# The recurrence's gates in the first mixer: issued behind each pair of convolutions, in main PSUM banks, with tanh and a second exponential

## The chip, the cores and the metric

One core of one Trainium2 chip runs the program. The metric is device time in microseconds (us), the median of three runs. PE is the matmul engine, DVE the vector engine, ACT the engine of activation functions, POOL the general one (GpSimd), SP the queue that issues loads.

## The reference

Two decoder layers on 256 tokens of width 1024, all in float32. Layer 0 has a mixer of two branches (a gated linear recurrence, RG-LRU, and sliding-window attention) and a dense SwiGLU; layer 1 has a gated DeltaNet and a mixture of 8 experts. The change lies in the recurrence of layer 0, whose width is 512:

```python
xc = causal_depthwise_conv(xb, conv_w) + conv_b          # width 4
r  = sigmoid(blockdiag(w_a) @ xc + b_a)
gi = sigmoid(blockdiag(w_i) @ xc + b_i)
log_a = -8 * r * softplus(-lam)
a  = exp(log_a)
u  = sqrt(-expm1(2 * log_a)) * (gi * xc)
h[t] = a[t] * h[t-1] + u[t]                              # scan over tokens
y_lru = h * gelu(gate)
```

The attention branch takes q, k and v from the same input projection; both branches feed one output projection.

## The kernel before, in words

Activations stand channels by tokens. Every float32 operand is split in two parts (`split`, L165 to L167): ACT rounds a copy (`hi`, L166) and DVE subtracts it (`lo`, L167); a product is then three fast matmuls (`mm3`, L220). Weights arrive in tiles of 1 MB and are split the same way, one ACT and one DVE instruction of 128x2048 each. Two `hi` buffers hold the split weights in turn, so the split of the next tile but one waits until PE has done with the older tile.

The input projection of layer 0 runs as six items in the order `kv x0 x1 qq g0 g1` (`L0ORD`): keys and values, the two halves of the recurrence's input, queries, the two halves of its output gate. `x0` and `x1` are 48 matmuls of 256 columns each (`chan_unit`), `qq` is 48 of 512 columns. The result of `x0` holds two of the recurrence's four blocks of 128 channels (blocks 0 and 1), that of `x1` blocks 2 and 3. Each block goes through `conv`: one ACT Identity (L400) and three DVE taps (L402) into the tile `xc`. Here "gate" means the pair of small block-diagonal products of one block (`wgate`), and not the items `g0` and `g1`.

Smaller chains are generators in the list `sides`; `pump` advances them between matmuls. In the kernel before, `lru_side` joins that list when both halves are convolved: per block it issues the gate's two matmuls into a bank of the four `ps` banks, two Sigmoids, later the Exp and Tanh, products on POOL, one Sqrt over all blocks, products on POOL, and the scan on DVE (L603). Its result times the GeLU gate `ge` is split into `yth` and `ytl`, which the output projection reads first. A scheduler places all instructions on their engines' queues by priority and by its own estimates of time, so that the order on a queue is not that of the source. `xc`, `rr`, `gi`, `aa` and `th_` are whole tiles for all four blocks. The tiles of matrix results are `pm` (four main banks, from `mbank`) and `ps` (four side banks, from `bank`).

Of the kernel before, what the change touches and what calls it, by code (L numbers as in the profile page):

```python
# [62 lines left out]
def body(ctx, tc, T, out, hrows):  # L63
# [357 lines left out]
    with tc.tile_pool(name="l0", bufs=1) as lp:  # L421
# [156 lines left out]

        def lru_side():
            for i in range(HB):  # L580
                b = bank([P, 2, S])
                for g in range(2):
                    mm(b[:, g, :], wgate[:, g, i, :], xc[:, i, :], True, True)
                nc.scalar.activation(rr[:, i, :], b[:, 0, :], AF.Sigmoid, bias=lruc[:, i, 5:6])
                sig = nc.scalar.activation(gi[:, i, :], b[:, 1, :], AF.Sigmoid, bias=lruc[:, i, 6:7])
                if i < HB - 1:
                    yield
            with tc.issue_after(sig.ins):
                for i in range(HB):
                    nc.scalar.activation(aa[:, i, :], rr[:, i, :], AF.Exp, scale=spn[:, i:i + 1])  # L590
                    nc.scalar.activation(th_[:, i, :], rr[:, i, :], AF.Tanh, scale=spp[:, i:i + 1])
            yield
            for i in range(HB):
                nc.gpsimd.tensor_tensor(gi[:, i, :], gi[:, i, :], xc[:, i, :], ALU.mult)
                nc.gpsimd.tensor_tensor(rr[:, i, :], aa[:, i, :], aa[:, i, :], ALU.mult)
                nc.vector.scalar_tensor_tensor(th_[:, i, :], rr[:, i, :], 1.0, th_[:, i, :], op0=ALU.add, op1=ALU.mult)
                if i % 2:
                    yield
            nc.scalar.activation(th_, th_, AF.Sqrt)
            yield  # L600
            for i in range(HB):
                nc.gpsimd.tensor_tensor(gi[:, i, :], gi[:, i, :], th_[:, i, :], ALU.mult)
                nc.vector.tensor_tensor_scan(xc[:, i, :], aa[:, i, :], gi[:, i, :], 0.0, op0=ALU.mult, op1=ALU.add)  # L603
                if i % 2:
                    yield
            while not {"g0", "g1"} <= done:
                yield
            for u in range(2):
                sl = slice(2 * u, 2 * u + 2)
                nc.vector.scalar_tensor_tensor(ge[:, sl], ge[:, sl], 0.5, xc[:, sl], op0=ALU.mult, op1=ALU.mult)  # L610
# [7 lines left out]
        nc.vector.tensor_scalar(spn, sp, -8.0, None, op0=ALU.mult)  # L618
        spp = lp.tile([P, HB], F32, name="spp")
        nc.vector.tensor_scalar(spp, sp, 8.0, None, op0=ALU.mult)  # L620
        done = set()
        for item in L0ORD.split():
# [9 lines left out]
            elif item[0] == "x":  # L632
                b = chan_unit(hnT)
                for m in range(2):
                    i = 2 * u + m
                    conv(b[:, m, :], lruc[:, i, 0:4], xc[:, i, :], bias=lruc[:, i, 4:5])
                done.add(item)
# [834 lines left out]
```

## Time and profile before

| what | value |
|---|---|
| median of 3 runs | 1514.45 us (1514.42 to 1515.34) |
| the profiled execution, its own time | 1516.59 us |
| its span, first to last instruction | 1514.5 us |
| mean granted TensorE clock | 0.982 |
| PE busy | 1470.5 us, 97% of the span |
| ACT, DVE, POOL busy | 950.1, 1178.7, 124.3 us |

A timeline row reads: start, duration, engine, line, operation, output <- inputs, shapes, how many instructions are merged in the row, and in brackets how long the engine had been idle before it and which instruction ended that. The granted clock is a share of full speed; 1.00 is 2.4 GHz, 0.50 is 1.2 GHz.

### The profile page before, as it was taken

The numbers are of one execution on the slowest core, as the hardware profiler recorded it, in microseconds if no ns is written. First come the engines' busy times: TensorE is split into PE (matmuls) and PEld (weight loads), VectorE is DVE, ScalarE is ACT, GpSimd is POOL, SyncE is SP. The second block draws the span as 40 slices with busy tenths as digits, with TensorE's granted clock in tenths as the row PEclk, the third lists the DMA queues.
The fourth block names the chain that finished last, engine by engine and source line by source line (L and its number), as shares of the span: only waits on it lengthen the run. The fifth ranks groups of instructions, "written<-read, shape, count | busy, mean of one in ns | idle before, by whom it ended". The sixth has DMA issues, their size and how long they took to land. (4 is left out here: it accounts for less than half of the span.)

```text
span 1514.5 us, 19426 instructions
## 1 busy us (share of the span) xinstructions
PE 1470.5 (97%) x7702; PEld 1246.4 (82%) x7702; DVE 1178.7 (78%) x1030; ACT 950.1 (63%) x894; POOL 124.3 (8%) x168
## 2 busy tenths in 40 slices
PE   8899999989998999999999999999999999999997
PEld 7679999969987778888888888888888888888886
DVE  5855444466867678888888888888898888888886
ACT  5744434345645467667767677767777667776674
POOL 2500000042010020010000000001001001001000
PEclk9899999989999899999999999999999999999999
DMA  8124455433330788999999999999999999999991
GB/s 319 68 111 154 172 190 188 180 140 112 140 138 4 300 324 344 373 357 391 375 370 383 367 372 382 379 372 376 383 365 372 386 372 358 391 375 370 385 355 17
DMA packets 65617, 435.79 MB, mean 288 GB/s; under 512 B 8304, under 2 KB 9584, under 8 KB 14320
## 3 DMA queue, kind: packets, MB, share of 16 engines
q1 hardware_dynamic: 62208, 426.62, 73.4%
q0 software_dynamic: 3312, 7.87, 2.2%
q8 instruction: 62, 1.02, 0.3%
q14 instruction: 35, 0.29, 0.0%
HBM read 428.17 MB, written 6.29 MB: 287 GB/s over the span
## 5 line engine op out<-in xcount | busy, mean ns | idle before, releaser
L220 PE MATMUL pm<-hi,X 128*128 128x512 f32 x1776 | 577.7, 396 | 0.0
L166 ACT ACTIVATE hi<-raw_raw 128x2048 fp32r<-128x2048 f32 (+2 forms) x199 | 352.4, 1810 | 146.1 <-PE pm L220 102.7
L167 DVE TENSOR_TENSOR lo_raw<-raw_raw,hi 128x2048 fp32r<-128x2048 f32 (+2 forms) x150 | 318.2, 2127 | 123.4 <-ACT hi L166 118.0
L220 PEld LDWEIGHTS pm<-hi,X 128*128 128x128 f32 x1776 | 333.6, 188 | 74.1
L167 DVE TENSOR_TENSOR lo_mraw<-raw_mraw,hi 128x2048 fp32r<-128x2048 f32 (+1 forms) x157 | 348.6, 2222 | 38.5 <-ACT hi L166 29.5
L166 ACT ACTIVATE hi<-raw_mraw 128x2048 fp32r<-128x2048 f32 (+1 forms) x186 | 330.3, 1852 | 0.0
L220 PE MATMUL ps<-hi,mG 128*128 128x512 f32 x864 | 277.9, 392 | 0.0
L220 PE MATMUL pm<-lo_mraw,X 128*128 128x512 f32 x496 | 193.9, 393 | 0.0
L220 PEld LDWEIGHTS ps<-hi,mG 128*128 128x128 f32 x864 | 162.2, 188 | 37.2
L220 PE MATMUL pm<-thi,hi 128*128 128x256 f32 x608 | 173.7, 286 | 1.2 <-ACT thi L166 1.2
L220 PE MATMUL pm<-tlo,hi 128*128 128x256 f32 x608 | 173.7, 286 | 0.3 <-DVE tlo L167 0.3
L220 PE MATMUL pm<-thi,lo_raw 128*128 128x256 f32 x592 | 169.2, 286 | 0.0
L1262 ACT ACTIVATE ms<-pm 128x512 f32<-128x512 f32 x56 | 33.5, 597 | 208.5 <-PE pm L220 172.5
L220 PE MATMUL pm<-lo_raw,X 128*128 128x512 f32 x348 | 136.8, 393 | 0.0
L220 PEld LDWEIGHTS pm<-thi,hi 128*128 128x128 f32 x608 | 118.0, 194 | 3.1 <-ACT thi L166 1.5
L220 PEld LDWEIGHTS pm<-tlo,hi 128*128 128x128 f32 x608 | 117.9, 194 | 1.7 <-DVE tlo L167 0.6
L220 PEld LDWEIGHTS pm<-thi,lo_raw 128*128 128x128 f32 x592 | 114.9, 194 | 0.7 <-issue 0.5
L220 PEld LDWEIGHTS pm<-lo_mraw,X 128*128 128x128 f32 x496 | 93.3, 188 | 19.6
L220 PE MATMUL ps<-lo_mraw,mG 128*128 128x512 f32 x268 | 100.8, 394 | 0.7 <-ACT mG L166 0.7
L1277 POOL DMA_INDIRECT out<-Y,si x16 | 29.9, 1868 | 635.2 <-ACT Y L1276 634.5
L220 PEld LDWEIGHTS pm<-lo_raw,X 128*128 128x128 f32 x348 | 65.5, 188 | 13.7
L220 PE MATMUL ps<-lo_raw,mG 128*128 128x512 f32 x180 | 70.8, 393 | 0.0
(376 smaller groups left out, 1815.4 us busy)
## 6 DMA issues: line engine op xcount, KB each, us to landing
raw_mraw<-in_moe SPq DMA_DIRECT2D x182, 1024.0 KB, 6.0
raw_raw<-in_moe SPq DMA_DIRECT2D x127, 1024.0 KB, 6.3
raw_tlo<-in_moe SPq DMA_DIRECT2D x26, 1024.0 KB, 6.5
raw_raw<-in_w SPq DMA_DIRECT2D x21, 1024.0 KB, 5.0
raw_raw<-in_fg SPq DMA_DIRECT2D x11, 1024.0 KB, 4.8
raw_raw<-in_fu SPq DMA_DIRECT2D x11, 1024.0 KB, 4.8
raw_raw<-in_fd SPq DMA_DIRECT2D x11, 1024.0 KB, 4.8
raw_raw<-in_w0o SPq DMA_DIRECT2D x4, 1024.0 KB, 4.8
```

The lines of the kernel that those rows point to most:

```text
L166: a = nc.scalar.activation(hi, src, AF.Copy)
L167: return a.ins, nc.vector.tensor_tensor(lo, src, hi.bitcast(F32), ALU.subtract).ins
L220: pe_last[0] = nc.tensor.matmul(o, l, r, start=start, stop=stop).ins
L1262: nc.scalar.activation(s, b, AF.Silu)
L1277: nc.gpsimd.indirect_dma_start(out[n], bass.IndirectOffsetOnAxis(ap=si, axis=0), Y[:, sl], None, bounds_check=ROWS - 1, oob_is_err=True, c ...
```

## The change

`lru_gates(i)` replaces the first half of `lru_side`. It is called for both blocks of a half right behind their convolutions, at a raised priority (`SPRI` is 20). Its matmuls write to main banks. Sigmoid(v) is written as (1 + tanh(v/2))/2; the factors of one half go into the constants (`spn`, `spp`, `hb`, the 0.25 at the end). The squared decay, before a product on POOL, is a second exponential. The products with `xc` and with the root go to DVE.

```diff
--- before.py
+++ after.py
@@ -576,30 +576,24 @@
         th_ = lp.tile([P, HB, S], F32, name="th_")
         ge = lp.tile([P, HB, S], F32, name="ge")
 
+        def lru_gates(i):
+            b = mbank([P, 2, S])
+            for g in range(2):
+                mm(b[:, g, :], wgate[:, g, i, :], xc[:, i, :], True, True)
+
+            nc.scalar.activation(rr[:, i, :], b[:, 0, :], AF.Tanh, scale=0.5, bias=hb[:, i, 0:1])
+            nc.scalar.activation(gi[:, i, :], b[:, 1, :], AF.Tanh, scale=0.5, bias=hb[:, i, 1:2])
+            nc.scalar.activation(th_[:, i, :], rr[:, i, :], AF.Tanh, scale=spp[:, i:i + 1], bias=spp[:, i:i + 1])
+            nc.scalar.activation(aa[:, i, :], rr[:, i, :], AF.Exp, scale=spn[:, i:i + 1], bias=spn[:, i:i + 1])
+            nc.scalar.activation(rr[:, i, :], rr[:, i, :], AF.Exp, scale=spn2[:, i:i + 1], bias=spn2[:, i:i + 1])
+            nc.vector.scalar_tensor_tensor(th_[:, i, :], rr[:, i, :], 1.0, th_[:, i, :], op0=ALU.add, op1=ALU.mult)
+            nc.vector.scalar_tensor_tensor(gi[:, i, :], gi[:, i, :], 1.0, xc[:, i, :], op0=ALU.add, op1=ALU.mult)
+
         def lru_side():
+            nc.scalar.activation(th_, th_, AF.Sqrt)
+            yield
             for i in range(HB):
-                b = bank([P, 2, S])
-                for g in range(2):
-                    mm(b[:, g, :], wgate[:, g, i, :], xc[:, i, :], True, True)
-                nc.scalar.activation(rr[:, i, :], b[:, 0, :], AF.Sigmoid, bias=lruc[:, i, 5:6])
-                sig = nc.scalar.activation(gi[:, i, :], b[:, 1, :], AF.Sigmoid, bias=lruc[:, i, 6:7])
-                if i < HB - 1:
-                    yield
-            with tc.issue_after(sig.ins):
-                for i in range(HB):
-                    nc.scalar.activation(aa[:, i, :], rr[:, i, :], AF.Exp, scale=spn[:, i:i + 1])
-                    nc.scalar.activation(th_[:, i, :], rr[:, i, :], AF.Tanh, scale=spp[:, i:i + 1])
-            yield
-            for i in range(HB):
-                nc.gpsimd.tensor_tensor(gi[:, i, :], gi[:, i, :], xc[:, i, :], ALU.mult)
-                nc.gpsimd.tensor_tensor(rr[:, i, :], aa[:, i, :], aa[:, i, :], ALU.mult)
-                nc.vector.scalar_tensor_tensor(th_[:, i, :], rr[:, i, :], 1.0, th_[:, i, :], op0=ALU.add, op1=ALU.mult)
-                if i % 2:
-                    yield
-            nc.scalar.activation(th_, th_, AF.Sqrt)
-            yield
-            for i in range(HB):
-                nc.gpsimd.tensor_tensor(gi[:, i, :], gi[:, i, :], th_[:, i, :], ALU.mult)
+                nc.vector.tensor_tensor(gi[:, i, :], gi[:, i, :], th_[:, i, :], ALU.mult)
                 nc.vector.tensor_tensor_scan(xc[:, i, :], aa[:, i, :], gi[:, i, :], 0.0, op0=ALU.mult, op1=ALU.add)
                 if i % 2:
                     yield
@@ -607,7 +601,7 @@
                 yield
             for u in range(2):
                 sl = slice(2 * u, 2 * u + 2)
-                nc.vector.scalar_tensor_tensor(ge[:, sl], ge[:, sl], 0.5, xc[:, sl], op0=ALU.mult, op1=ALU.mult)
+                nc.vector.scalar_tensor_tensor(ge[:, sl], ge[:, sl], 0.25, xc[:, sl], op0=ALU.mult, op1=ALU.mult)
                 split(yth[:, sl, :], ytl[:, sl, :], ge[:, sl])
             done.add("lru")
 
@@ -615,9 +609,13 @@
         nc.vector.tensor_scalar(nlam, lruc[:, :, 7], -1.0, None, op0=ALU.mult)
         sp = softplus(nlam, [P, HB])
         spn = lp.tile([P, HB], F32, name="spn")
-        nc.vector.tensor_scalar(spn, sp, -8.0, None, op0=ALU.mult)
+        nc.vector.tensor_scalar(spn, sp, -4.0, None, op0=ALU.mult)
+        spn2 = lp.tile([P, HB], F32, name="spn2")
+        nc.vector.tensor_scalar(spn2, sp, -8.0, None, op0=ALU.mult)
         spp = lp.tile([P, HB], F32, name="spp")
-        nc.vector.tensor_scalar(spp, sp, 8.0, None, op0=ALU.mult)
+        nc.vector.tensor_scalar(spp, sp, 4.0, None, op0=ALU.mult)
+        hb = lp.tile([P, HB, 2], F32, name="hb")
+        nc.vector.tensor_scalar(hb, lruc[:, :, 5:7], 0.5, None, op0=ALU.mult)
         done = set()
         for item in L0ORD.split():
             u = int(item[1]) if item[1].isdigit() else 0
@@ -634,6 +632,9 @@
                 for m in range(2):
                     i = 2 * u + m
                     conv(b[:, m, :], lruc[:, i, 0:4], xc[:, i, :], bias=lruc[:, i, 4:5])
+                with tc.high_priority(offset=SPRI):
+                    for m in range(2):
+                        lru_gates(2 * u + m)
                 done.add(item)
                 if {"x0", "x1"} <= done:
                     sides.append(lru_side())
```

**What the order of the instructions shows, at three places.** First PE at the end of `x0` and the start of `x1`. `pm_312` is the bank of `x0`, `pm_411` that of `x1`. Before:

```order
L220 MATMUL pm_312<-thi_77,hi_196 128x256
L220 MATMUL pm_312<-tlo_78,hi_196 128x256
L220 MATMUL pm_312<-thi_77,lo_raw_35_195 128x256
L220 MATMUL pm_411<-thi_77,hi_307 128x256
L220 MATMUL pm_411<-tlo_78,hi_307 128x256
```

With the change `pm_316` is the bank of `x0`, `pm_435` that of `x1`; `pm_409` and `pm_419` are the gates of blocks 0 and 1, and L485 transposes the second tile of keys:

```order
L220 MATMUL pm_316<-tlo_78,hi_196 128x256
L220 MATMUL pm_316<-thi_77,lo_raw_35_195 128x256
L485 MATMUL ps_397<-c_ident_81,ro_365 128x128
L220 MATMUL pm_409<-xc,c_wgate_127 128x256 x2
L220 MATMUL pm_419<-xc,c_wgate_127 128x256 x2
L220 MATMUL pm_435<-thi_77,hi_311 128x256
L220 MATMUL pm_435<-tlo_78,hi_311 128x256
```

The gates of blocks 0 and 1 now stand between the last matmul of `x0` and the first of `x1`. Before, no gate stood ahead of `qq`.

Second PE at the start of `qq`. Before, `qq` (banks `pm_468` and `pm_469`) followed `x1` at once, and the first gate (`ps_494`) stood within it:

```order
L220 MATMUL pm_469<-hi_406,tlo_78 128x512
L220 MATMUL pm_469<-hi_406,thi_77 128x512
L220 MATMUL ps_494<-xc,c_wgate_127 128x256 x2
L220 MATMUL pm_469<-lo_raw_65_405,thi_77 128x512
L220 MATMUL pm_469<-hi_406,tlo_78 128x512
```

With the change `pm_492` and `pm_502` are the gates of blocks 2 and 3, and `pm_512` is the first bank of `qq`:

```order
L220 MATMUL pm_435<-tlo_78,hi_311 128x256
L220 MATMUL pm_435<-thi_77,lo_raw_48_310 128x256
L220 MATMUL pm_492<-xc,c_wgate_127 128x256 x2
L220 MATMUL pm_502<-xc,c_wgate_127 128x256 x2
L220 MATMUL pm_512<-hi_430,thi_77 128x512
L220 MATMUL pm_512<-lo_raw_67_429,thi_77 128x512
L220 MATMUL pm_512<-hi_430,tlo_78 128x512
```

All four gates now stand ahead of `qq`, the last two between the end of `x1` and its first matmul. In the kernel before, the first bank of `qq` and the second took turns, half a weight at a time; with the change all 24 matmuls of the first bank stand ahead of the 24 of the second.

Third ACT around the convolution of blocks 2 and 3 (the two L400 rows from the bank of `x1`). `hi_471` (before) and `hi_515` (with the change) are the split of the second weight tile of `qq`. Before:

```order
L486 ACTIVATE kT<-ps_393 128x256
L166 ACTIVATE hi_471<-raw_kb_17_129 128x2048
L400 ACTIVATE xc<-pm_312,c_lruc_121 128x256
L400 ACTIVATE xc<-pm_411,c_lruc_121 128x256
L584 ACT_TABLE_LOAD
L584 ACTIVATE rr<-ps_494,c_lruc_121 128x256
L585 ACTIVATE gi<-ps_494,c_lruc_121 128x256
```

With the change:

```order
L587 ACTIVATE aa<-rr,spn 128x256
L588 ACTIVATE rr<-rr,spn_254 128x256
L166 ACTIVATE hi_515<-raw_kb_17_129 128x2048
L400 ACTIVATE xc<-pm_435,c_lruc_121 128x256 x2
L584 ACTIVATE rr<-pm_492,hb 128x256
L585 ACTIVATE gi<-pm_492,hb 128x256
```

The split of that weight stands ahead of both Identities of `x1` now, and on DVE its difference (L167) stands ahead of their taps. In both kernels the Identity of the second block of a half waits for the last tap of the first block, since both write the tile `xc`. On DVE the difference of the first weight of `qq` stands ahead of block 0's taps in both kernels.

## Rows read from the trace of the kernel before

**Rows 1.** The profile's page: busy time of each engine with its share of the span and its instructions, then the busy share of PE and its granted clock in 40 equal slices, in tenths.

```profile
PE 1470.5 (97%) x7702; PEld 1246.4 (82%) x7702; DVE 1178.7 (78%) x1030; ACT 950.1 (63%) x894; POOL 124.3 (8%) x168
PE   8899999989998999999999999999999999999997
PEclk9899999989999899999999999999999999999999
```

**Rows 2.** Busy time by stretches of 20 us: stretch, its length, then PE, weight loads, DVE, ACT and POOL busy, the granted clock, the share of the DMA engines and GB/s.

```profile
20.00:40.00 20.00, 19.89 (x144) 18.89 (x144) 14.55 (x38) 9.63 (x13) 4.43 (x12) 1.00 0.72 273
60.00:80.00 20.00, 13.19 (x65) 9.50 (x64) 17.78 (x33) 14.23 (x33) 8.22 (x8) 0.74 0.16 52
100.00:120.00 20.00, 14.72 (x71) 11.92 (x70) 13.98 (x18) 10.91 (x18) 1.99 (x6) 0.87 0.34 132
```

**Rows 3.** The timeline of PE over the last matmul of `x0` (28.55), the first of `x1` (28.67), the first two of `qq` (34.64), the first gate and the matmul behind it (38.98, 39.66), the last of `qq` and the first of `g0` (47.98, 48.20).

```profile
28.55 0.28 PE L220 MATMUL pm<-thi,lo_raw 128*128 128x256 f32 x1
28.67 0.28 PE L220 MATMUL pm<-thi,hi 128*128 128x256 f32 x1
...
34.64 0.63 PE L220 MATMUL pm<-hi,thi 128*128 128x512 f32 x2
...
38.98 1.03 PE L220 MATMUL ps<-xc,c_wgate 128*128 128x256 f32 x4
39.66 0.58 PE L220 MATMUL pm<-lo_raw,thi 128*128 128x512 f32 x1
...
47.98 0.39 PE L220 MATMUL pm<-hi,tlo 128*128 128x512 f32 x1
48.20 0.28 PE L220 MATMUL pm<-thi,hi 128*128 128x256 f32 x1
```

**Rows 4.** The timeline of ACT: the split of the first weight of `qq` (28.75), the Identity of block 0 (30.57), the split of the second weight of `qq` (34.77).

```profile
28.75 1.91 ACT L166 ACTIVATE hi<-raw_raw 128x2048 fp32r<-128x2048 f32 x1 [2.05 <-PE pm L220]
30.57 0.55 ACT L400 ACTIVATE xc<-pm,c_lruc 128x256 f32<-128x256 f32 x1
...
34.77 1.92 ACT L166 ACTIVATE hi<-raw_kb 128x2048 fp32r<-128x2048 f32 x1 [0.62 <-PE pm L220]
```

**Rows 5.** The timeline of DVE: the difference of the first weight of `qq`, the three taps of block 0, the difference of the second weight of `qq`.

```profile
30.70 2.54 DVE L167 TENSOR_TENSOR lo_raw<-raw_raw,hi 128x2048 fp32r<-128x2048 f32 x1 [1.18 <-ACT hi L166]
33.16 1.50 DVE L402 SCALAR_TENSOR_TENSOR xc<-pm,c_lruc,xc 128x255 f32<-128x255 f32 x3
...
36.71 2.29 DVE L167 TENSOR_TENSOR lo_raw<-raw_kb,hi 128x2048 fp32r<-128x2048 f32 x1 [2.05 <-ACT hi L166]
```

**Rows 6.** The timeline of PE around its two idle times of this stage, and one later matmul.

```profile
63.45 0.44 PE L505 MATMUL ps<-c_ident,ro 128*128 128x128 f32 x2
68.32 0.80 PE L220 MATMUL ps<-amr,identr 128*128 128x512 f32 x1 [4.43 <-ACT qT L507]
69.05 2.08 PE L220 MATMUL ps<-kT,qT 64*128 64x256 f32 x8
73.51 0.79 PE L220 MATMUL pm<-hi,yth 128*128 128x512 f32 x1 [2.38 <-ACT yth L166]
...
77.77 0.39 PE L220 MATMUL pm<-hi,yth 128*128 128x512 f32 x1
```

**Rows 7.** Stretches of half a microsecond in which the granted clock fell or rose, or PE started again; columns as in rows 2.

```profile
66.50:67.00 0.50, 0.00 (x0) 0.00 (x0) 0.50 (x2) 0.50 (x1) 0.50 (x1) 0.84 0.00 0
77.00:77.50 0.50, 0.50 (x6) 0.41 (x4) 0.24 (x3) 0.50 (x3) 0.00 (x0) 0.92 0.00 0
115.50:116.00 0.50, 0.32 (x1) 0.29 (x1) 0.50 (x2) 0.50 (x3) 0.00 (x0) 0.50 0.90 344
121.00:121.50 0.50, 0.50 (x5) 0.50 (x4) 0.50 (x1) 0.00 (x0) 0.00 (x0) 0.54 0.00 0
```

**Rows 8.** The timeline of all engines over the first idle time and up to the split of the recurrence's result: the two table loads, the Sqrt, POOL's products with the root, the Tanh of the GeLU, the queries' copy, the product of `ge` and `xc`, the split.

```profile
63.49 1.28 ACT L599 ACT_TABLE_LOAD   x1
64.78 1.06 ACT L599 ACTIVATE th__224<-th__224 128x1024 f32<-128x1024 f32 x1
65.86 1.28 ACT L647 ACT_TABLE_LOAD   x1
65.92 3.90 POOL L602 TENSOR_TENSOR gi<-gi,th__224 128x256 f32<-128x256 f32 x4 [1.45 <-ACT th__224 L599]
67.15 0.63 ACT L647 ACTIVATE ge<-ge 128x512 f32<-128x512 f32 x1
67.69 0.58 ACT L507 ACTIVATE qT<-ps 128x512 f32<-128x512 f32 x1
...
72.13 0.66 DVE L610 SCALAR_TENSOR_TENSOR ge<-ge,xc 128x512 f32<-128x512 f32 x1
...
72.83 0.63 ACT L166 ACTIVATE yth<-ge 128x512 fp32r<-128x512 f32 x1 [4.04 <-DVE ge L610]
```

**Rows 9.** Instructions by tile: line, engine, operation, how many, then least, median and greatest duration in ns, first and last start.

```profile
L590 ACT ACTIVATE aa<-rr,spn x4: 494/494/510, 54.5 to 56.9; 128x256 f32<-128x256 f32 x4
L594 POOL TENSOR_TENSOR gi<-gi,xc x4: 734/744/2797, 41.0 to 53.3; 128x256 f32<-128x256 f32 x4
L596 DVE SCALAR_TENSOR_TENSOR th__224<-rr,th__224 x4: 424/827/1508, 56.2 to 63.2; 128x256 f32<-128x256 f32 x4
```

## The prediction

> **What bounds the kernel now.** I read the page first: PE is busy for 97% of the span, so a change elsewhere counts only where PE waits, and the 40 slices show it full nearly everywhere [rows 1]. Then the stage that the change touches, in stretches of 20 us [rows 2]: from 20 to 40 us PE lacks 0.1 us; from 60 to 80 us it lacks 6.8 us and the clock is down to 0.74; the holes at 100 to 120 us belong to the next norm, which the change leaves alone. What is won or lost before 120 us arrives at the end: behind it PE is full again and each load waits for a buffer that PE's progress frees.
>
> The two holes at 60 to 80 us are the recurrence's. The first opens when the transposes end (63.45 + 0.44 = 63.89) and lasts 4.43 us, until the queries' copy; the second lasts 2.38 us, until `yth` [rows 6]. In the first, ACT does a table load, the Sqrt, another load and a Tanh before it reaches that copy; in the second, the chain is POOL's products with the root (3.90 us), the scan, the product with `ge` and the split [rows 8]. The clock fell at 66.84 (0.16 below full in half a microsecond is 0.16 us at half clock) and came back at 77.08 [rows 7].
>
> In front, PE is full because nothing waits there: `x0` ends at 28.83, `x1` starts at once (28.67), `qq` follows at 34.64 and the first gate comes only at 38.98, inside `qq` [rows 3]. That gate needs block 0's taps, which ended at 33.16 + 1.50 = 34.66 [rows 5]. PE spent those 5.8 us on `x1`.
>
> **What the change gives.** The gates' chains start earlier, and scan and root are done long before the output projection. I let both holes go: 4.43 + 2.38 = 6.8 us. PE's work between them and behind them ran at half clock: 68.32 to 71.13 and 73.51 to 77.08 [rows 6, 7], 6.4 us that would take 3.2. **Together 10.0 us gained**. What is late next there would be the GeLU's own chain, now without the recurrence in front of it.
>
> **What it costs: the first wait.** PE meets the gates of blocks 0 and 1 right behind `x0`, with all 48 matmuls of `x1` behind them. Block 0's Identity is at 30.57 behind a weight's split [rows 4], its taps end at 34.66 behind a difference of 2.54 us [rows 5]; neither moves. So PE stands from 28.83 to 34.66: 5.8 us (the key transposes in it are tiny). Gate 0 takes 39.66 - 38.98 = 0.68 us [rows 3]. Block 1's Identity waits for block 0's last tap: 0.55 [rows 4] and three taps of 1.50 [rows 5] put gate 1 at 36.71, another 1.4 us of standing. `x1` starts at 37.4 instead of 28.67 and, at 34.64 - 28.67 = 6.0 us less the transposes now ahead of it, ends at 43.2.
>
> **The second wait.** Gates 2 and 3 stand ahead of `qq`. The split of the second `qq` weight waits for the buffer that `x1` holds to its end, and the Identities of blocks 2 and 3 are queued behind it on ACT, their taps behind its difference on DVE. From 43.2: split 1.92 [rows 4], difference 2.29, taps 1.50 [rows 5], so gate 2 at 48.9: 5.7 us of standing. Then Identity and taps of block 3, 2.05 us, of which gate 2 fills 0.68: 1.4 us. Before, the same split and difference lay under the first half of `qq`, which needs only its first weight. **Standing together: 5.8 + 1.4 + 5.7 + 1.4 = 14.3 us**, say 14.0 without the transposes. The gates' own matmuls were on PE before and are not counted.
>
> **The clock** is unknown for these waits, so I bound it. In this trace it fell 2.95 us into the idle time that began at 63.89, and stayed down until 3.6 us after PE's restart at 73.51 in one place (77.08) and 5.8 us after its restart at 115.68 in another (121.46) [rows 6, 7]. Both new waits are near 6 us. Each would leave 3.6 to 5.8 us of work at half clock, 1.8 to 2.9 us lost; twice that is 3.6 to 5.8 us. The bound below is nothing. The first hole, 4.43 us without work, is the nearest row, and it lost the clock; I take 4.6.
>
> **A late weight.** `g0` needs the buffer of the first `qq` weight. With one bank of `qq` after the other, it is free only half-way through the second bank: 12 matmuls of 0.23 us before the end, 2.8 us, against 1.91 + 2.29 = 4.2 us for split and difference [rows 4, 5]. PE has two matmuls and the transposes to do meanwhile: 1.0 us lost. The bounds are nothing and 1.4.
>
> **The rest at nothing.** Two of five table loads go, 1.28 us of ACT each [rows 8], and four exponentials of 0.49 come [rows 9]; ACT's chains of five per block run while PE does `x1` or `qq`. Eight products of some 0.75 us leave POOL [rows 9], four squares too; eight come to DVE at 0.42 to 0.8, the times of its like product [rows 9], under `qq`. If that cover went, 2 to 5 us of DVE would delay the queries' norms, which PE meets only in `g0`. The main banks turn faster (eight tiles in four banks instead of four), but each is read out before its turn comes: `qq`'s second bank was `x1`'s, read by taps that gate 3 has waited for anyway. SP's order is the same.
>
> **Sum:** 14.0 + 4.6 + 1.0 - 10.0 = **9.6 us slower**. The profiled execution took 1516.59 us with a span of 1514.5, 2.1 us above the median of 1514.45; the sum puts a like execution at 1526.2 and the median at **1524.0 us**.
>
> **The rule weighed.** The idle PE at 63.89 had only matmuls behind it that needed the same copy or later work, so no row here shows what PE does with a ready matmul behind a waiting one [rows 6]. The Trainium skill, TensorE: Matmul & The Clock Gate, section "Step-by-step: what each phase is for", states that matmuls stay in program order and that only weight loads are pulled ahead. By that rule the sum is +9.6; if `x1` could pass the gates, it would be the -10.0 of the second rival.
>
> **The rivals.**
> - *The holes come back.* Softmax, GeLU and the late `yth` chain then wait as long as before, and only the cost stays: +19.6, 1534 us. For it: ACT and DVE are the fuller engines at 60 to 80 us [rows 2]. Against: the loads, the Sqrt and POOL's 3.90 us leave just that chain [rows 8]. Chance 0.07.
> - *PE is not held.* If `x1` starts at 28.67 all the same and the gates slip in when their taps are done, only the gain is left: -10.0, 1504.5 us, faster. This decides at one point: whether the first 256-column matmul of `x1` starts before gate 0. For it, only that no row shows the contrary; against it, the first gate of the kernel before ran exactly where PE's order has it [rows 3]. Chance 0.05.
> - *The second wait is hidden.* If the Identity of block 2 began when its half of `x1` is done, its taps would lie under the other half: 7.1 us and one fall of the clock less (2.3), so about +0.2 us, 1514.7, no change. Against: both its engines have the weight's split and difference ahead of it, and those wait for the end of `x1`. Chance 0.04.
> - *The clock holds.* Waits of 6 us with a few transposes and gates in them leave it at full: +5.0, 1519.5 us. Against: rows 7. Chance 0.07.
>
> **How the numbers follow.** My forecast has 0.77, with its own range from 1521 (clock losses at the small end, less than a full second wait) to 1528 (both losses large, the late weight at 1.4, a fifth of the gain missing). The range for 8 in 10 takes in the clock that holds, and ends at **1519.0 and 1528.0 us**; left out are the first three rivals, 0.16. A measurement of this kernel tells about 0.2% from no change, 3.0 us. Slower by more: 0.77 + 0.07 + 0.07 = 0.91; the same: 0.04; faster: 0.05.
>
> **What would show it.** In the profile after: PE idle until gate 0, near 34.7, released by DVE's `xc`; `x1` from about 37; a second idle time of 5 to 6 us at the end of `x1`, again released by `xc`; the clock at 0.50 in both; `qq` ending near 67; no wait for `qT` or `yth` over 1 us; three table loads before 100 us. Wrong if `x1` starts near 29, if the second wait is under 2 us, or if PE still stands 4 us before the output projection.

## The result and the profile after

The changed kernel takes **1529.38 us** (median of four runs, 1528.41 to 1530.25) against 1514.89 us for the kernel before on the same chip (1514.42 to 1515.57): slower, ratio 1.0094, 95% interval 1.0082 to 1.0105. The prediction was 1524.0 us in a range of 1519.0 to 1528.0: the direction and the two waits came true, the time lies outside the range, 5 us above the forecast. The profiled execution took 1529.2 us, its span is 1527.3 us.

The page of the changed kernel, the same lines as [rows 1]:

```profile
PE 1475.6 (97%) x7702; PEld 1247.9 (82%) x7702; DVE 1179.9 (77%) x1040; ACT 951.7 (62%) x896; POOL 113.3 (7%) x156
...
PE   7798999989999899999999999999999999999997
...
PEclk8899999989999899999999999999999999999999
```

PE's share is 97% as before, at the same count of matmuls; the average hides the stage. What the slices show is their beginning: 7 7 9 8 9 9 9 in place of 8 8 9 9 9 9 9, and a clock of 8 8 in place of 9 8. By stretches of 20 us, columns as in [rows 2]:

```profile
20.00:40.00 20.00, 14.27 (x93) 12.68 (x92) 13.22 (x37) 10.16 (x18) 4.41 (x12) 0.83 0.57 221
40.00:60.00 20.00, 14.17 (x66) 11.61 (x65) 8.45 (x16) 10.73 (x17) 0.00 (x0) 0.83 0.16 54
60.00:80.00 20.00, 17.35 (x110) 15.97 (x109) 15.14 (x20) 8.94 (x8) 7.66 (x7) 0.91 0.15 53
```

Between 20 and 60 us PE lacks 5.7 + 5.8 us where it lacked 0.1 before, and the clock is at 0.83; the holes of 60 to 80 us, 6.8 us before, have shrunk to 2.7 us, and they are other holes. The timeline of PE shows which. The first row is the transpose of the second tile of keys, the next row holds the gates of blocks 0 and 1 (eight records, two for each matmul), then come the first matmul of `x1`, the gates of blocks 2 and 3, and the start of `g0`:

```profile
30.12 0.33 PE L485 MATMUL ps<-c_ident,ro 128*128 128x128 f32 x1 [2.29 <-POOL ro L479]
33.74 4.24 PE L220 MATMUL pm<-xc,c_wgate 128*128 128x256 f32 x8 [3.29 <-issue]
37.42 0.72 PE L220 MATMUL pm<-thi,hi 128*128 128x256 f32 x1
...
49.49 4.19 PE L220 MATMUL pm<-xc,c_wgate 128*128 128x256 f32 x8 [5.72 <-DVE xc L402]
...
65.21 0.28 PE L220 MATMUL pm<-tlo,hi 128*128 128x256 f32 x1
66.50 0.66 PE L505 MATMUL ps<-c_ident,ro 128*128 128x128 f32 x4 [1.01 <-POOL ro L466]
68.80 0.58 PE L220 MATMUL pm<-thi,lo_kb 128*128 128x256 f32 x1 [1.64 <-DVE lo_kb L167]
```

The last matmul of `x0` ended at 27.83 (it began at 27.55, before at 28.55). Gate 0 is at 33.74, 5.91 us later, with the 48 matmuls of `x1` behind it: [rows 3] had `x1` start at once. "Issue" as releaser means only that no wait of PE's own is shown, since PE's transpose lies between. DVE's rows show what the gate needed, block 0's taps behind the difference of a weight:

```profile
29.69 2.52 DVE L167 TENSOR_TENSOR lo_raw<-raw_raw,hi 128x2048 fp32r<-128x2048 f32 x1 [1.18 <-ACT hi L166]
32.13 1.50 DVE L402 SCALAR_TENSOR_TENSOR xc<-pm,c_lruc,xc 128x255 f32<-128x255 f32 x3
```

The taps ended at 33.63, 0.1 us ahead of the gate. The second wait is 5.72 us, released by DVE's `xc`. What DVE and ACT did in it (the row of the split, of block 2's Identity, of the weight's difference, of the three taps of block 2, of block 3's Identity):

```profile
43.69 1.91 ACT L166 ACTIVATE hi<-raw_kb 128x2048 fp32r<-128x2048 f32 x1 [3.08 <-PE pm L220]
...
45.50 0.55 ACT L400 ACTIVATE xc<-pm,c_lruc 128x256 f32<-128x256 f32 x1
45.63 2.29 DVE L167 TENSOR_TENSOR lo_raw<-raw_kb,hi 128x2048 fp32r<-128x2048 f32 x1 [4.56 <-ACT hi L166]
47.84 1.51 DVE L402 SCALAR_TENSOR_TENSOR xc<-pm,c_lruc,xc 128x255 f32<-128x255 f32 x3
49.38 0.56 ACT L400 ACTIVATE xc<-pm,c_lruc 128x256 f32<-128x256 f32 x1 [3.33 <-DVE xc L402]
```

It is the predicted queue, to a few hundredths: the weight's split of 1.91 first, then the Identity; the difference of 2.29 first, then the taps. The granted clock in both waits and at a third place, columns as in [rows 2]:

```profile
32.00:34.00 2.00, 0.26 (x1) 0.29 (x2) 1.56 (x4) 0.33 (x1) 0.00 (x0) 0.50 0.02 8
48.00:50.00 2.00, 0.51 (x1) 0.50 (x2) 1.30 (x4) 0.56 (x1) 0.00 (x0) 0.54 0.00 0
70.00:72.00 2.00, 2.00 (x12) 2.00 (x11) 2.00 (x3) 0.00 (x0) 0.29 (x2) 0.50 0.00 0
```

0.50 is the lower of the two levels; in the second row it fell some 0.2 us after the stretch began. The third stretch is not one that the prediction named: it is in `g0`, where PE is busy all the time. `g0` got two matmuls out (65.09, 65.21), then PE stood 1.01 us for the query transposes and 1.64 us for the weight's difference, the last two rows of PE's timeline above. The engines that were late there, with the squares of the first query tile on ACT, the recurrence's scans and the sum of those squares on DVE ahead of them:

```profile
59.85 0.60 ACT L454 ACTIVATE sq<-pm 128x512 f32<-128x512 f32 x1 [1.12 <-PE pm L220]
...
60.12 2.43 DVE L597 TENSOR_TENSOR_SCAN xc<-aa,gi 128x256 f32<-128x256 f32 x4
62.46 0.66 DVE L456 TENSOR_REDUCE s<-sq 128x8 f32<-128x512 f32 x1
...
65.17 1.28 POOL L466 TENSOR_TENSOR ro<-ro,rp 128x512 f32<-128x512 f32 x1
...
65.25 1.23 DVE L497 TENSOR_SCALAR s<-s 128x8 f32<-128x8 f32 x1 [0.86 <-POOL s L270]
...
66.47 2.28 DVE L167 TENSOR_TENSOR lo_kb<-raw_kb,hi 128x2048 fp32r<-128x2048 f32 x1
```

DVE's `L497` is a product of 128x8 numbers; it waited 0.86 us for POOL's power and then took 1.23 us, until 66.48, 0.03 us after the end of POOL's sum of the rope (65.17 + 1.28 = 66.45). Its twin `L499` right behind it took 0.16. Only then came the difference of `g0`'s weight. The whole norm was late before that: its squares were ready at 60.45, but DVE did the recurrence's products with the root (58.77) and its four scans first and began the sum of the squares at 62.46, 2.0 us later.

The output projection starts at 85.73 without a wait (before 73.51, after 2.38 us of one), and the feed-forward's first matmul is at 128.60 (before 115.68). From there the two traces keep their distance: 12.9 us there, 12.8 us at the end of the span.

### The profile page after: what moved, and what is told of

It reads as the page before. It is cut to its first block, busy times and chain, and to the rows that moved or that the text cites. A ratio compares the mean times of both kernels' runs of the same rounds, so it can differ in the third digit from the quotient of the medians.

```text
span 1527.3 us, 19431 instructions
## 1 busy us (share of the span) xinstructions
PE 1475.6 (97%) x7702; PEld 1247.9 (82%) x7702; DVE 1179.9 (77%) x1040; ACT 951.7 (62%) x896; POOL 113.3 (7%) x156
## 5 line engine op out<-in xcount | busy, mean ns | idle before, releaser
L167 DVE TENSOR_TENSOR lo_raw<-raw_raw,hi 128x2048 fp32r<-128x2048 f32 (+2 forms) x150 | 317.6, 2123 | 133.8 <-ACT hi L166 128.4
L167 DVE TENSOR_TENSOR lo_mraw<-raw_mraw,hi 128x2048 fp32r<-128x2048 f32 (+1 forms) x157 | 348.5, 2222 | 38.5 <-ACT hi L166 26.1
```

What stands on the lines that cost most here:

```text
L167: return a.ins, nc.vector.tensor_tensor(lo, src, hi.bitcast(F32), ALU.subtract).ins
```

## The experiments

In each run below, the **stage** is the time from the start of `x0`'s last matmul to the feed-forward's first, the part that the change touches: 115.68 - 28.55 = 87.13 us before, 128.60 - 27.55 = 101.05 after (+13.9). What lies ahead of it varies by 1 us between profiled executions (27.55 to 28.55): in the five that are there by 27.68 the clock had been at 0.50 for 3.4 us somewhere between 13 and 18 us, in the other nine for 6.8 us between 10 and 20. The stage column is the difference to before in the profiled execution; the times are medians, the ratios are against the kernel before on the same chip.

| run | median us | ratio, 95% | stage |
|---|---|---|---|
| changed kernel | 1529.38 | 1.0094, 1.0082 to 1.0105 | +13.9 |
| e1_arith | 1516.17 | 1.0004, 0.9994 to 1.0014 | +2.4 |
| e2_place | 1532.51 | 1.0114, 1.0097 to 1.0130 | +16.1 |
| e3_first | 1526.72 | 1.0078, 1.0061 to 1.0095 | +11.1 |
| e4_second | 1521.40 | 1.0041, 1.0027 to 1.0055 | +6.5 |
| e5_conv_first | 1521.94 | 1.0044, 1.0028 to 1.0061 | +6.2 |
| e6_scalars | 1530.32 | 1.0095, 1.0079 to 1.0112 | +16.7 |
| e7_fill | 1525.94 | 1.0072, 1.0055 to 1.0089 | +10.9 |
| e8_before_conv | 1515.27 | 0.9997, 0.9987 to 1.0006 | -0.2 |
| e9_late | 1525.66 | 1.0067, 1.0051 to 1.0084 | +10.5 |
| e10_side_half | 1512.07 | 0.9978, 0.9969 to 0.9988 | -4.5 |
| e11_side_all | 1512.10 | 0.9975, 0.9965 to 0.9985 | -4.8 |
| e12_conv_late | 1523.40 | 1.0057, 1.0040 to 1.0074 | +9.7 |

**Arithmetic or place: e1 and e2.** The change has two halves, and each was run alone. e1, in the changed kernel:

```
-            b = mbank([P, 2, S])
+            b = bank([P, 2, S])
...
         def lru_side():
+            for i in range(HB):
+                lru_gates(i)
+                if i < HB - 1:
+                    yield
             nc.scalar.activation(th_, th_, AF.Sqrt)
...
-                with tc.high_priority(offset=SPRI):
-                    for m in range(2):
-                        lru_gates(2 * u + m)
```

> The new arithmetic alone: tanh, the squared decay by an exponential and the products on DVE stay, but the four gates are back in the recurrence's side step, in the ps banks, so that they stand inside qq again. Theory 'place' (the two waits and the clock that falls in them, 17 us in the trace, come from where the gates stand): no PE wait at the end of x0 or of x1, and the holes at 60 to 80 us shrink by POOL's 3.90 us and a table load, so 1 to 6 us faster than before, 1509 to 1514 us. Rival 'arithmetic' (five ACT functions a block and eight more DVE products delay the weight of g0 and the queries' norms): slower than before by 3 us or more, 1518 us and up, with PE idle at the start of g0.

No change: 1.0004. Neither theory had it: the waits are gone, and so is the gain. The timeline of e1 over a weight's difference, the product of `ge` and `xc`, and the output projection's first matmul:

```profile
69.50 2.27 DVE L167 TENSOR_TENSOR lo_raw<-raw_raw,hi 128x2048 fp32r<-128x2048 f32 x1
71.70 0.68 DVE L608 SCALAR_TENSOR_TENSOR ge<-ge,xc 128x512 f32<-128x512 f32 x1
...
73.10 0.79 PE L220 MATMUL pm<-hi,yth 128*128 128x512 f32 x1 [8.67 <-ACT yth L166]
```

One hole of 8.67 us stands where there were two of 4.43 and 2.38 [rows 6]. The root still comes after the GeLU's first Tanh (60.66) and pays its own table load (61.80); and the product that `yth` needs is queued behind a weight's difference. POOL's 3.90 us left the chain, the queue on DVE took their place: the projection starts 45.0 us behind `x0` in both kernels. In the stage e1 loses 2.4 us, all of them behind that start; in the profiled execution it wins them back between 300 and 560 us, in the second mixer, where the same PE matmul goes from 1.9 us later to 1.1 us sooner. A few instructions stand in another order there; no run tells which of them does it.

e2 is the other half: the kernel before, with

```
+        def lru_gates(i):
+            b = mbank([P, 2, S])
...
+            nc.scalar.activation(rr[:, i, :], b[:, 0, :], AF.Sigmoid, bias=lruc[:, i, 5:6])
+            sigs.append(nc.scalar.activation(gi[:, i, :], b[:, 1, :], AF.Sigmoid, bias=lruc[:, i, 6:7]))
...
+                with tc.high_priority(offset=SPRI):
+                    for m in range(2):
+                        lru_gates(2 * u + m)
```

and the rest of the side step as it was.

> The new place alone: the arithmetic of the kernel before (sigmoids, squared decay and products on POOL), but each half's gates right behind its convolution in main banks. Theory 'place': the same two waits as in the changed kernel, 5.9 + 1.4 and 5.7 + 1.4 us with 2.8 us of slow clock, 17 us; the chain starts earlier too, so part of the holes goes, 5 to 10 us: 1522 to 1530 us. Rival 'arithmetic': within 3 us of before, 1512 to 1518 us.

1.0114: the place is the whole loss, and by the stage more. Its waits ahead of gate 0 and gate 2 are those of the changed kernel (3.29 behind the transposes, 5.78). The arithmetic goes with some 2 us less of the stage when the gates are early (13.9 against 16.1), and as much more when they are late (e1); part of either may be the clock, which in e2 comes back from its third fall at 76.3 us, in the changed kernel at 72.1, and in e1 from the fall in its hole at 79.1, before at 77.1. Place and bank changed together here: no run has the early gates in `ps` banks, and what speaks for the place is that both waits end when the taps into `xc` do.

**Which wait: e3 and e4.** In the changed kernel, the gates of one half only stay behind their convolution (`if u == 0:` or `if u == 1:` ahead of the call), the others go to the side step, in the ps banks.

> The changed kernel with only the gates of blocks 0 and 1 behind their convolution; those of blocks 2 and 3 are in the side step. Theory 'place': only the first wait stays, 7.3 us of standing and about 1.4 us of slow clock, so the end of qq comes 8 to 9 us later than before; blocks 2 and 3 end as late as before, so 0 to 6 us of the holes go: 1518 to 1524 us. Rival 'the second wait is what costs': within 3 us of before.

> The changed kernel with only the gates of blocks 2 and 3 behind their convolution; those of blocks 0 and 1 are in the side step and come out just ahead of them. Theory 'place': PE meets all four gates at the end of x1 and stands there 5.7 + 1.4 us with 1.4 to 2 us of slow clock, the end of qq 8 to 9 us late; the chain is early, so the holes go as in the changed kernel, 7 to 10 us, less the late weight of g0, up to 4 us: 1514 to 1520 us. Rival 'the first wait is all of it': 1505 to 1512 us.

e3 is above its range, +11.1 in the stage: the first wait, and a hole of 6.00 us ahead of the output projection, because the chain of blocks 2 and 3 is as late as ever. e4 at 1521.4 is 1.4 us above its range. Its gate 0 passed at 34.45 without a wait, so PE met three gates at the end of `x1` and not four. PE in e4, at gate 1 and at the start of `g0`:

```profile
41.47 2.04 PE L220 MATMUL ps<-xc,c_wgate 128*128 128x256 f32 x4 [5.92 <-DVE xc L402]
...
59.55 0.66 PE L505 MATMUL ps<-c_ident,ro 128*128 128x128 f32 x4 [2.16 <-POOL ro L466]
61.77 0.39 PE L220 MATMUL pm<-thi,lo_kb 128*128 128x256 f32 x1 [1.57 <-DVE lo_kb L167]
```

One wait of 5.92 us and the third wait, 2.16 + 1.57 us: with the chain early and the first half unhindered, 6.5 us are still lost. So each wait costs by itself. Of the two runs, the one with the second wait has the third; e3 has none at the start of `g0`.

**What the waits are made of: e5.** In the changed kernel, `conv` returns its Identity and its last tap, and the weights' splits are queued behind them until `qq` is issued:

```
+                conv_last[:] = ids[1]
...
-                    split(hi[:, sl], lo[:, sl], raw[:, sl])
+                    with behind(conv_last):
+                        split(hi[:, sl], lo[:, sl], raw[:, sl])
```

> The changed kernel with one order turned round: the split of each following weight (ACT) and its difference (DVE) are queued behind the Identities and the taps of the half that has just ended, not ahead of them. Theory (the waits are not the convolution's own time but the weight's split and difference in front of it on ACT and DVE): each of the two waits falls from 5.7 to about 2.2 us, with 1.4 us more for the second block each time, so 7 us of standing go, and of the 2.8 us of slow clock most goes too since no wait is 3 us long: 7 to 10 us less than the changed kernel, 1519 to 1523 us. Rival (the waits are the convolution's, or the weight is now late by as much): within 2 us of the changed kernel, 1527 to 1531 us.

1521.94 us, the stage 7.7 us shorter than the changed kernel's. PE in e5 at the key transposes, gate 1, gate 2 and gate 3:

```profile
30.13 0.33 PE L488 MATMUL ps<-c_ident,ro 128*128 128x128 f32 x1 [2.30 <-POOL ro L482]
...
32.28 1.86 PE L222 MATMUL pm<-xc,c_wgate 128*128 128x256 f32 x4 [0.18 <-DVE xc L404]
...
42.19 1.10 PE L222 MATMUL pm<-xc,c_wgate 128*128 128x256 f32 x4 [2.30 <-DVE xc L404]
44.34 2.04 PE L222 MATMUL pm<-xc,c_wgate 128*128 128x256 f32 x4 [1.05 <-DVE xc L404]
```

Gate 0 follows the transposes at 30.29, without a wait of its own: the taps are no longer what it waits for. The second wait is 2.30 us. So 3.4 us of either wait were another piece of work that happened to stand first in the queue. The time is in the forecast's range, but the price of the new place is then still 6 us: the clock fell all the same after waits of 2.3 us (0.54 in 32 to 34, 0.52 in 44 to 46), which the expectation had excluded.

**The clock: e7.** In the changed kernel, 22 matmuls on a constant ahead of the first gate of each half and 4 ahead of the second.

> The changed kernel with PE kept busy in the two waits: 22 matmuls of 128x512 on a constant between the end of x0 (and of x1) and the first gate behind it, 4 between the two gates; they are written to a bank that nobody reads. It takes the clock's share alone: the standing stays. Theory (2.8 us of the 17 are slow clock, at the gates and the first matmuls of x1 and qq): the clock stays at 1.00 from 28 to 55 us and the time falls by 2 to 3 us, 1526 to 1527.5 us. Rival (what follows waits for weights anyway, or the clock costs nothing): 1529 us or more.

By stretches of 20 us, columns as in [rows 2]:

```profile
20.00:40.00 20.00, 18.77 (x128) 17.24 (x127) 13.49 (x39) 10.75 (x19) 4.52 (x12) 1.00 0.55 222
40.00:60.00 20.00, 18.91 (x96) 15.92 (x95) 10.08 (x19) 10.59 (x16) 0.00 (x0) 1.00 0.15 54
60.00:80.00 20.00, 16.67 (x128) 14.99 (x127) 15.69 (x21) 9.82 (x9) 8.57 (x7) 1.00 0.15 53
```

The clock is at 1.00 throughout, and the time is 1525.94 us, 3.4 us less, a little more than forecast. Up to the last matmul of `qq` e7 is 2.6 us ahead of the changed kernel (34.72 against 37.32 us behind `x0`'s last). The standing did not change: gate 0 comes 6.20 us behind `x0`'s last for 6.19, gate 2 6.00 us behind `x1`'s last in both. So 2.6 us is the clock's share in the two waits. The rest is the third fall, which did not come either, though the waits at the start of `g0` are longer here:

```profile
64.68 0.66 PE L505 MATMUL ps<-c_ident,ro 128*128 128x128 f32 x4 [1.70 <-POOL ro L466]
66.97 0.39 PE L220 MATMUL pm<-thi,lo_kb 128*128 128x256 f32 x1 [1.64 <-DVE lo_kb L167]
```

1.70 + 1.64 us of standing and the clock holds; in the changed kernel 1.01 + 1.64 us, and it fell.

**The start of `g0`: e6 and e9.** e6 moves the two small products to POOL:

```
-            nc.vector.tensor_scalar(rs, rq, 0.125, None, op0=ALU.mult)
+            nc.gpsimd.tensor_scalar(rs, rq, 0.125, None, op0=ALU.mult)
```

(and `nrs` likewise).

> The changed kernel with the two tiny products of the queries' norm (L497, L499) on POOL, behind whose power they wait, and no longer on DVE ahead of the difference of g0's weight. Theory (the difference at 66.47 us was late since DVE stood for those products, its input was ready at 64.49): the difference starts 1 to 2 us sooner, and PE's third fall of the clock goes if the wait becomes short enough: 1 to 3.5 us less than the changed kernel, 1526 to 1528.5 us. Rival (the difference is late for its hi part, which waits for a buffer): no change, 1528.5 to 1530 us.

The time, 1530.32, is 0.3 us above the rival's range, but the rival's reason is not the right one either: the difference did start sooner, and PE waited longer. DVE's two differences and POOL's sum, then the PE row of the transposes:

```profile
65.41 2.28 DVE L167 TENSOR_TENSOR lo_kb<-raw_kb,hi 128x2048 fp32r<-128x2048 f32 x1
...
66.28 4.74 POOL L466 TENSOR_TENSOR ro<-ro,rp 128x512 f32<-128x512 f32 x1
...
67.61 2.28 DVE L167 TENSOR_TENSOR lo_raw<-raw_raw,hi 128x2048 fp32r<-128x2048 f32 x1
```

```profile
71.08 1.11 PE L505 MATMUL ps<-c_ident,ro 128*128 128x128 f32 x4 [5.41 <-POOL ro L466]
```

POOL's sum, 1.28 us in the changed kernel, took 4.74 and ended at 71.02, 1.1 us after the second difference. PE meets the transposes ahead of `g0`'s third matmul, so now they are late. This execution is the longest of its four (1531.52; the shortest 1529.22). The Trainium skill, SBUF — State Buffer, section "Who interferes with whom", has it that a `tensor_tensor` with both inputs in SBUF contends with GpSimd's reads, and that the issue order decides who is blocked; the sum behind the differences agrees. `L497` behind the sum is a `tensor_scalar`, of which that sentence does not speak.

e9 therefore takes the sum away as well:

```
-            nc.gpsimd.tensor_tensor(o, o, r2, ALU.add)
+            nc.vector.tensor_tensor(o, o, r2, ALU.add)
```

> The changed kernel with the sum of the query rope (L466) on DVE and the two tiny products (L497, L499) on POOL, so that no long POOL instruction lies beside the weight's difference. In the changed kernel the product L497 ended 0.03 us after POOL's sum (66.48 and 66.45); with only the products moved, the sum took 4.74 us beside two differences. Theory (DVE's big instructions and POOL's sum keep each other waiting, and that is what made PE stand 2.65 us at the start of g0): sum 0.7 us on DVE, difference about 1 us sooner, PE stands 1 to 1.5 us and its clock stays up: 1.5 to 3 us less than the changed kernel, 1526.5 to 1528 us. Rival (DVE is too full there: what POOL did only comes on top): 1529 to 1531 us.

1525.66 us, 3.4 us less in the stage than the changed kernel, better than forecast. The sum and the difference on DVE, and `g0`'s third matmul:

```profile
64.32 0.69 DVE L466 TENSOR_TENSOR ro<-ro,rp 128x512 f32<-128x512 f32 x1
...
64.93 2.29 DVE L167 TENSOR_TENSOR lo_kb<-raw_kb,hi 128x2048 fp32r<-128x2048 f32 x1
...
67.27 0.38 PE L220 MATMUL pm<-thi,lo_kb 128*128 128x256 f32 x1 [1.31 <-DVE lo_kb L167]
```

The sum costs DVE 0.69 us and the difference starts at 64.93; PE stands 1.31 us once, and the clock stays up. From the start of `g0` on, e9 takes 60.3 us to the feed-forward, the changed kernel 63.5.

**The kernel before with e5's order: e8.**

> The kernel before, arithmetic and place of the gates unchanged, with the same one order turned round as in e5: splits and differences of the following weights behind the convolution. Theory (in the kernel before the same order made the first gate late, at 38.98 us, and with it the chain that opens the two holes at 60 to 80 us): the gates come 2 to 4 us sooner, part of the 6.8 us of holes and 3 us of slow clock goes: 3 to 9 us faster than before, 1506 to 1512 us. Rival (the weight that qq waits for becomes late by the same 4 us): 1514 us or more, with PE idle at the start or in the middle of qq.

No change. The gates come at 34.11 and 41.33 (before 38.98 and later), the output projection starts 2.5 us sooner behind `x0`, though PE stands 1.51 us for POOL's sum (2.89 us here, beside a difference) and 2.95 us for the queries' copy. But from there to the feed-forward it takes 44.42 us for 42.17 with the same matmuls, so the gain is gone again. The theory failed: an earlier recurrence alone does not move the stage.

**All of it: e10, e11 and e12.** e10 is the new arithmetic with e5's order, e9's two moves, and a side step for each half in place of the direct call:

```
-                with tc.high_priority(offset=SPRI):
-                    for m in range(2):
-                        lru_gates(2 * u + m)
+                sides.append(gate_side(u))
```

where `gate_side` yields twice, then issues one gate a turn, in ps banks; e11 keeps the one side step of e1.

> The new arithmetic, the convolution ahead of the following weight's split (as in e5), the rope's sum on DVE and its two products on POOL (as in e9), and the gates of each half in a side step of their own, behind some matmuls of the next weight, in the ps banks: PE has ready work ahead of every gate. Theory (the new place was right in bringing the chain forward and wrong in holding PE for it): no wait over 1 us at the ends of x0 and x1, all gates by 43 us, no wait at the start of g0, the holes at 60 to 80 us gone or under 2 us: 6 to 10 us faster than before, 1505 to 1509 us. Rival (as in the runs e1 and e8 the time comes back as another wait ahead of the output projection): 1512 to 1516 us.

> As e10_side_half, but with all four gates in the one side step that begins when both halves are done, so that the first two come at the end of x1 and not within it. Theory: the chain of blocks 0 and 1 is some 2 us later than in e10 and still far ahead of its use, so the same time within 2 us, 1505 to 1510 us. Rival: 1512 to 1516 us.

1512.07 and 1512.10 us: faster than both kernels, ratio 0.9978 (0.9969 to 0.9988) and 0.9975 (0.9965 to 0.9985). They miss the theory's ranges (up to 1509 and 1510) and lie at the lower edge of the rival's (1512 to 1516); some waits did come back ahead of the projection, the longest 1.24 us for `yth`. The gates of e10 are at 33.45, 35.38 and from 41.72 on, none with a wait. By stretches of 20 us:

```profile
20.00:40.00 20.00, 19.91 (x144) 19.00 (x145) 15.36 (x49) 11.53 (x21) 3.47 (x10) 1.00 0.72 273
40.00:60.00 20.00, 20.00 (x134) 18.36 (x133) 18.43 (x27) 17.42 (x22) 6.26 (x9) 1.00 0.15 54
60.00:80.00 20.00, 17.08 (x95) 12.20 (x95) 16.49 (x42) 12.54 (x37) 2.78 (x1) 1.00 0.14 52
```

PE lacks 0.1 and 0.0 us in the first two, 2.9 us in the third, in pieces of at most 1.24, and the clock is at 1.00. The stage is 4.5 us shorter; some 1.1 us of that are lost again in the second mixer.

> The changed kernel with its gates where they are, and both remedies together: the convolution ahead of the following weight's split (e5, 1521.9 us) and the rope's sum on DVE with the products on POOL (e9). Theory: e5 still had a wait of 2.5 us for POOL's sum at the start of g0 with a slow clock behind it, and that goes: 2 to 4 us less than e5, 1518 to 1520 us, still slower than before by the two waits of some 2.3 + 1 us and their clock. Rival: as e5, 1521 to 1523 us.

1523.40 us: the forecast was wrong, and the time is 0.4 us above the rival's range too. The start of `g0` has no wait in e12, and the output projection starts 1.5 us sooner behind `x0` than in e5. But the stage is 3.5 us longer than e5's in the profiled executions, by the medians, each against its kernel before, 1.3 us. In `x1` the clock, which e5 has back at 1.00 from 34 us on, is still at the lower level here; and it fell twice more behind the projection's start, after a wait of 1.52 us for a softmax row (82.9 to 86.3 us) and after two short ones, 0.6 us together (103.4 to 106.8 us):

```profile
36.00:38.00 2.00, 2.00 (x11) 2.00 (x11) 0.83 (x3) 1.97 (x5) 0.00 (x0) 0.50 0.00 0
100.00:110.00 10.00, 9.38 (x50) 7.94 (x50) 5.90 (x8) 2.14 (x3) 0.00 (x0) 0.83 0.32 107
```

What was taken from one wait came back in others, in part as slow clock.

## Why the prediction was right and wrong

The mechanism was right: PE is held by its program order, both waits are where they were forecast, released by `xc`, and the two old holes are gone. The Trainium skill, TensorE: Matmul & The Clock Gate, section "Step-by-step: what each phase is for", whose rule the prediction weighed, says that matmuls stay in program order; the trace agrees: `x1` did not pass the gates (37.42, behind gate 0 at 33.74).

The sizes, by the prediction's own terms, for the stage of +13.9:

| term | predicted | measured | from |
|---|---|---|---|
| standing at the gates | 14.0 | 14.4 to 14.6 | 17.2 less the clock |
| slow clock of the two waits | 4.6 | 2.6 to 2.8 | e7; trace |
| late weight of `g0` | 1.0 | 4.2 | trace; e9's stage is 3.4 shorter |
| gain | -10.0 | -7.5 | trace |

The first two together: from `x0`'s end to `g0`'s start 65.09 - 27.83 = 37.26 us against 48.20 - 28.83 = 19.37 before, and 0.68 of the difference is gate 3, which only moved here: 17.2. The last two: from `g0`'s start to the feed-forward 63.51 us against 67.48, 4.0 less; without gate 3's 0.68 it is 3.3 = 7.5 - 4.2.

**The step that failed is "A late weight".** Its bounds were nothing and 1.4; it cost 4.2 us: 1.01 + 1.64 of standing and some 1.5 of slow clock, since `g0`'s matmuls followed each other at 0.21 us in place of 0.12 until 72.0. The prediction priced the split and the difference of the weight and let PE do "the transposes meanwhile". It did not ask what stood on DVE ahead of the difference (the queries' norm with its wait for POOL), nor who frees the transposes (POOL's sum). And it had the reason why the norm was late: "The rest at nothing" says that 2 to 5 us of DVE work "would delay the queries' norms, which PE meets only in `g0`" if `qq` did not cover it, and prices that at nothing. The cover went in part: the recurrence's products and scans, now early, held the norm for 2.0 us. No run moves these alone, so how much of the 4.2 us they make is open; in e10, where they stand behind the first norm (the sum of its squares at 48.25, the products from 55.45 on), nothing waits at the start of `g0`. The order of `qq`'s banks is part of it: in the changed kernel, e2, e4, e6, e7 and e9 one bank follows the other, and all but e6, where the transposes were later still, stood 1.3 to 1.8 us for that difference; where the banks take turns (before, e1, e3, e5, e8, e10 to e12) none did. The prediction used that order for the buffer alone. e9 shows most of the step mended: PE stands 1.31 us for 2.65, within the prediction's bounds, the clock holds, and the stage is 3.4 us shorter.

**The gain was 2.5 us too large.** The 6.8 us of holes are gone and the slow clock behind them too. But attention work now falls into other places. The scores of two heads, in PE's timeline after, then twice those of one head:

```profile
84.66 1.13 PE L220 MATMUL ps<-kT,qT 64*128 64x256 f32 x8
...
91.55 1.13 PE L220 MATMUL ps<-kT,qT 64*128 64x256 f32 x4
...
93.03 1.13 PE L220 MATMUL ps<-kT,qT 64*128 64x256 f32 x4
```

Eight records of two heads taking turns in two banks take as long as four of one head: 1.06 us lost once more than before, where all came by eights. Some 1.1 us are small gaps between the output projection and the transposes near 90 and 105 us, 0.4 us longer rows of the values' product. "Holes gone" was priced as time gained; part of it is other work in a worse order.

**The clock was 2 us too dear.** It came back 4.2 us behind gate 0 (37.9) and 5.5 us behind gate 2 (55.0), inside the bounds of 3.6 to 5.8 us, but that was not all work: gate 0 ran slow while gate 1 had to wait for block 1's taps anyway (34.27 + 1.51 = 35.78, gate 1 at 35.93). Had the other terms been right, the forecast would have come out too slow; the errors partly cancelled, and that was luck.

The rivals: "PE is not held" and "the second wait is hidden" are excluded by the two waits, "the clock holds" by the 0.50 and 0.54 in both, "the holes come back" by the start of the output projection without a wait. The tell-tales came out: gate 0 at 33.74 for 34.7, `x1` from 37.42 for 37, the second wait 5.72 for 5 to 6, `qq`'s end at 65.1 for 67. What remains open is 0.6 us between the stage's +13.9 and the medians' +14.5: the start, ahead of the stage, varies by more than that. Another 0.4 us of the miss is the median of the kernel before, 1514.89 here and 1514.45 in the prediction.

## What to carry to other kernels

Work that a queue has to meet in order belongs behind other ready work, not right behind what produces its input: the same gates held PE for 14 us in one place and not at all in the other (e10). When a wait is found, ask what stands ahead of its releaser: here 3.4 us of each wait were a weight's split that could as well have come second (e5). And price a hole that goes by what will fill it, and a weight by the whole queue ahead of it, on every engine that it crosses.

## What was not expected of the hardware

- A small DVE product took 1.23 us in place of 0.16 beside a POOL sum, and that sum 4.74 in place of 1.28 beside two DVE differences: in these rows the one ended within 0.03 us of the other, or 1.1 us after it. In e9 the two small products, 128x8, took 2.12 and 2.26 us on POOL beside the differences; in e10 the first two took 0.27 and 0.23.
- The clock fell after 1.01 + 1.64 us of standing in the changed kernel and held after 1.70 + 1.64 us at the same place in e7. In e5 it fell after waits of 2.3 us, in e12 after one of 1.52 and later after two of 0.6 us together, while e10 kept it through one of 1.24. No run here shows what tells these apart.
- Score matmuls of 64 rows from two heads in two banks ran two at a time, eight records in 1.13 us; four of one head in one bank took 1.13 us too. The Trainium skill, TensorEngine Tiling (Array Packing), section "Theoretical Speedup", gives up to 2 for a dimension of 64 or less; the rows agree.
